# Prompt attention on one core: full-row products with the low parts of the keys, P and its values one point later, sinks copied by ScalarE

## The chip, the cores and the metric

The kernel runs on one core of a Trainium2 chip. The metric is the device time of one execution in microseconds. The core has TensorE (matrix products; PE for the products, PEld for the loads of their stationary operand), VectorE (DVE), ScalarE (ACT), GpSimd (POOL) and SyncE (SP, which issues most of the transfers). They run side by side, each through its own instructions in program order, and wait for each other by semaphores.

## The reference

One layer of a decoder: a prompt of 2048 tokens with 1024 features, and 32 sample rows (8 sequences of 4 tokens) that look at caches. One input projection gives queries, keys and values of two attention branches, and two gates:

```python
qa, ka, va, qb, kb, vb, ga, gb = split(x @ w_in)      # rotary positions on q and k
# A: window 128, 8 query heads, 2 key heads of 64, one learned sink per head
s = where(mask, qa @ ka.T * 64 ** -0.5, -1e30)
m = maximum(max(s), sink)
oa = exp(s - m) / (sum(exp(s - m)) + exp(sink - m)) @ va
# B: three groups of 4 heads, (window, dilation) = (128, 1), (512, 4), (2048, 16)
ob = sum over groups of weight * softmax(qb @ kb.T * 64 ** -0.5) @ vb
x = LN(a * x + (sig(ga) * (oa @ w_a) + sig(gb) * (ob @ w_b)) @ w_o)
x = LN(a * x + (gelu(conv3(x @ w_u)) * (x @ w_v)) @ w_down)
```

In blocks of 128 tokens each query block looks at its own key block and the one before it. In the dilated groups a block consists of tokens 4 or 16 apart; the blocks of the third group, and each fourth of the second, have no block before them.

## The kernel before

All of it is float32. A product of two float32 operands is made as three products of split operands: hi · hi, lo · hi and hi · lo, where hi is ScalarE's rounded copy and lo the difference, made by VectorE (in branch A's splits of x by POOL).

**Phases.** Phase 1 projects and runs the prompt attention (to about 1158 us of the profile), then the gates and the attention of the sample rows (to about 1392 us); phases 2 and 3 are the output projection and the feed-forward.

**Slots.** Phase 1 is a row of slots, one for each tile of 128 tokens and each kind: B0, B1, B2 (the three groups of branch B), A, and G (gates). Each kind has 16 prompt slots (i = 0 to 15) and one of the sample rows (i = 16), which comes last except in G. A slot (`slot`, L352) makes 4 units of 256 columns, 8 steps of 128 rows and 3 products each: 96 products on L379. After every 12 of them there is a *point*, so that a slot has eight. At a point the slot calls `adv` (L381), which runs the next step of every attention job in flight, the newest first; the half projections that are done are taken out of PSUM (`late`, with the rotary arithmetic of `rope`, L427 to L435) at point 6 (point 5 in A) and after the last point:

```python
371                for kh in range(2):
...
381                    self.adv()
382                    if late is not None and (u, kh) == evac_at:
383                        late()
384                        late = None
...
406        if kind[0] == "B":
407            self.drain()
408        late()
```

At points 3 and 7 of B slots (`adv_bg`) one step of the cached-key products of the sample rows also runs on VectorE (L796, L799): 16 steps for each group, in slots 2 to 9 of the next kind (for the third group in A). At point 2 the next tile of x is split (`make_xs`: hi on ScalarE, L41, lo on VectorE, in A on POOL, L42). In B0 the tile of x is transposed there too.

**A job of branch B** (`attn_b`, L622) belongs to tile i and runs in slot i + 1. Its steps, one a point:

1. transposes of q (L630) and of k (L634, into the one bank of `psO`); `split_q` makes the stationary tiles qT[x] (L591, L593): hi in the 64 partitions a head comes in, lo in the other 64; `split_k` makes kH[x], hi twice above each other (L604, L606), and kL, the low parts (L608);
2. split of the values (`split_v`, L442, L445);
3. scores (`qk`, L617 and L619) for two heads of each pair, and the softmax of both pairs (`softmax_pair`: masked maximum L548, its scaled negative nm L552, exponentials L554);
4. nothing;
5. and 6. transposes of the exponentials P (L564), and their split PT (L41 on ScalarE, L42 on VectorE);
7. and 8. products with the values (L658), the first into the bank of `psO`, the second into one of three `psT` banks; `both` adds the two halves of the partitions into O (copy on ScalarE L572, sum on VectorE L573), POOL adds hi and lo (L661), and POOL's queue stores O to d_ob (L662).

With eight steps and eight points a job of branch B ends in its slot, and `drain` finds nothing to run in a plain slot.

The scores:

```python
617                nc.tensor.matmul(dst[x], lhsT=qT[x][:, qi], rhs=self.kH[x][:, ki, sl, :], start=True, stop=False)
618            for x, here, there in self.HALF:
619                nc.tensor.matmul(dst[x], lhsT=qT[x][here, qi], rhs=self.kL[here, ki, sl, :], start=False, stop=True)
```

L617 contracts over 128 rows, (hi + lo of q) · hi of k. L619 contracts over the 64 rows of one half, hi of q · lo of k; its two products lie in different halves of the array. A call makes two of each for each of two rounds r: eight products.

**A job of branch A** (`attn_a`, L665) has twelve steps and lasts one and a half slots, so two jobs are in flight. It calls `qk` twice, at points 3 and 5, and has four softmaxes: two at point 3, one at point 5, one at point 8. Each takes the sink as one more key: L692 copies two sink values (`sk8`) behind the scores in P on VectorE, then come the masked maxima (L694), nm (L697) and the exponentials (L699). P's transposes come at points 5 and 7, and at points 1 and 2 of the next slot; O (tile OA) is collected over points 1 to 4 of the next slot.

**Buffers.** P, PT: two each. O and OA: one tile in a pool of its own. `buf` (L306) is a shared ring of ten tiles of 128 × 512: raw weights and x, rotary temporaries, gates on their way out, cached keys.

Of the kernel before, what the change touches and what calls it, by code (L numbers as in the profile page):

```python
# [7 lines left out]
F32 = mybir.dt.float32  # L8
# [26 lines left out]
class Net:  # L35
# [19 lines left out]
    def unit_list(self):  # L55
        a = self.a
        w_in = a["w_in"][0].rearrange("(k p) n -> p k n", p=128)

        def win(c0):
            return unit(w_in[:, :, c0:c0 + 256])  # L60

        def unit(src):
            """pieces of 512 columns: (place in the unit, source)"""
            kk, n = src.shape[1:]
            if n > 512:
                ps = [((slice(k, k + 1), slice(c, c + 512)), src[:, k:k + 1, c:c + 512]) for k in range(kk) for c in range(0, n, 512)]
            else:
                d = 512 // n
                ps = [((slice(k, min(k + d, kk)), slice(0, n)), src[:, k:min(k + d, kk)]) for k in range(0, kk, d)]
            return kk, n, ps  # L70

        def pair(u, v):
            return 8, 256, [((slice(k, k + 4), slice(c, c + 128)), x[:, k:k + 4]) for c, x in ((0, u), (128, v)) for k in (0, 4)]

        gate = iter(range(8))
        us = []
        for g in range(3):
            us += [win(768 + g * 256), win(1536 + g * 256), win(2304 + g * 256)]
            us.append(win(GATE0 + 256 * next(gate)))
        us += [win(0), win(256), win(512), win(GATE0 + 256 * next(gate))]  # L80
        us += [win(GATE0 + 256 * next(gate)) for _ in range(4)]
        bra = a["w_br_a"][0].rearrange("(k p) n -> p k n", p=128)
        brb = a["w_br_b"][0].rearrange("(k p) n -> p k n", p=128)
        wo = a["w_o"][0].rearrange("(k p) n -> p k n", p=128)
        wo = [unit(wo[:, :, c * 256:(c + 1) * 256]) for c in range(4)]
        us += wo + [unit(bra[:, :, 0:512]), unit(brb), unit(bra[:, :, 512:1024])]
        wup = a["w_up"][0].rearrange("(k p) n -> p k n", p=128)
        wdn = a["w_down"][0].rearrange("(k p) n -> p k n", p=128)
        for _ in GROUPS:
            for ti, (j0, nj) in enumerate(THIRDS):  # L90
                for j in range(j0 + (ti > 0), j0 + nj + (ti < 2)):
                    us.append(pair(wup[:, :, j * 128:(j + 1) * 128], wup[:, :, DFF + j * 128:DFF + (j + 1) * 128]))
                us += [unit(wdn[:, j0:j0 + nj, c * 256:(c + 1) * 256]) for c in range(4)]
        return us

    def prefetch(self, limit=None):
        """raw loads of the next pieces, as many as may wait"""
        if limit is not None:
            self.rawlim = limit
        while len(self.raws) < self.rawlim and self.loaded < self.loadcap and (self.units or self.pieces):  # L100
            self.load_piece()
            self.loaded += 1
# [18 lines left out]
    def unit_steps(self, dst=None, pool=False):  # L121
        """a unit's tile and the steps that fill it"""
        kk, n, np_ = self.shapes.pop(0)
        if dst is None:
            w = self.wp.tile([128, 2, 2048], F32R, tag="w", name="w")
            hi3, lo3 = [w[:, x, :kk * n].rearrange("p (k n) -> p k n", k=kk) for x in range(2)]
        else:
            hi3, lo3 = dst

        def step(q):  # L130
            e = self.nc.gpsimd if pool and q == 1 else None
            r3, _, _, _, (ks, cs) = self.raws.pop(0)
            self.split(hi3[:, ks, cs], lo3[:, ks, cs], r3, e)
            self.prefetch()

        return (hi3, lo3), [lambda q=q: step(q) for q in range(np_)]

# [39 lines left out]
    # ==== phase 1: projections and prompt attention =======================  # L177
# [174 lines left out]
    def slot(self, kind, i, t, xs, units, prep, after_unit, rp):  # L352
# [53 lines left out]
        if kind[0] == "B":  # L406
            self.drain()
# [29 lines left out]
    def split_v(self, src):  # L437
        """hi and lo of the values beside each other for each head, two heads to a tile"""
        vs = []
        for c in range(src.shape[1] // 128):  # L440
            v = self.at.tile([128, 2, 2, 64], F32R, tag="vr", name="vr", bufs=4)
            self.nc.scalar.activation(v[:, :, 0], src[:, c * 128:(c + 1) * 128].rearrange("p (v d) -> p v d", v=2), AF.Copy)  # L442
            vs.append(v)
        for c, v in enumerate(vs):
            self.nc.vector.tensor_tensor(v[:, :, 1], src[:, c * 128:(c + 1) * 128].rearrange("p (v d) -> p v d", v=2),  # L445
                                         v[:, :, 0].bitcast(F32), ALU.subtract)
        return vs
# [95 lines left out]
    def softmax_pair(self, sps, nk, mask, m, nm, den, cols, accum=True, init=None):  # L543
        """exp of two heads' scores; m, nm, den: [128, n] tiles, cols: their two columns"""
# [13 lines left out]
    def transpose_p(self, P, order):  # L558
        """hi and lo of the transposed exponentials"""
# [9 lines left out]
    def both(self, O, ops, x):  # L569
        """the sum of the products with hi and lo values, which come in the two halves of the partitions"""  # L570
# [5 lines left out]
    def keys(self, n, has_prev):  # L576
        """slots of the ring, mask, number of key blocks and whether this tile's come first"""
# [7 lines left out]
    def split_q(self, q3):  # L585
        """hi and lo of a head's queries above each other; the hi half is the half that the head comes in"""
# [9 lines left out]
    def split_k(self, k3, cur):  # L596
        """hi of a head's keys twice above each other, and lo in the half that the head comes in"""
        nc = self.nc
        n = k3.shape[1]
        if not hasattr(self, "kH"):  # L600
            self.kH = [self.at1.tile([128, 2, 2, 128], F32R, name="kH%d" % x) for x in range(2)]
            self.kL = self.at1.tile([128, 2, 2, 128], F32R, name="kL")
# [4 lines left out]
        for x, here, there in self.HALF:  # L607
            nc.vector.tensor_tensor(self.kL[here, :n, cur], k3[here], self.kH[x][here, :n, cur].bitcast(F32), ALU.subtract)  # L608

    def qk(self, qT, sl, nk, pairs):  # L610
        """scores of two head pairs: one bank for each half of the partitions"""
        nc = self.nc
        tiles = [self.psS.tile([128, 512], F32, tag="s", name="pss") for _ in range(2)]
        for r, (qi, ki) in enumerate(pairs):
# [3 lines left out]
            for x, here, there in self.HALF:  # L618
                nc.tensor.matmul(dst[x], lhsT=qT[x][here, qi], rhs=self.kL[here, ki, sl, :], start=False, stop=True)  # L619
        return tiles  # L620

    def attn_b(self, kind, i, t):  # L622
# [24 lines left out]
        PTs = []  # L647
        for x in range(2):
            yield
            PTs.append(self.transpose_p(Ps[x], [(c, b) for c in range(2) for b in range(nb)]))  # L650
        O = self.at1.tile([128, 512], F32, tag="O", name="O")
# [13 lines left out]
    def attn_a(self, t):  # L665
# [22 lines left out]
        def softmax(r, x, sps):  # L688
            """exponentials of heads 4x + 2r and the next, the sink as one more key"""
            c = 4 * x + 2 * r  # L690
            P = self.at.tile([128, 2, 257], F32, tag="P", name="P")
            nc.vector.tensor_copy(P[:, :, nk], self.sk8[:, c:c + 2])  # L692
# [43 lines left out]
        O = self.at1.tile([128, 512], F32, tag="O", name="OA")  # L736
# [11 lines left out]
    def store_rec(self):  # L748
        """1 / denominator of branch A, one row for each tile and head"""
# [15 lines left out]
    def sample_scores(self, g):  # L765
        """products of the sample queries of one group with its cached keys: [slot, (h, b, t)]"""
# [35 lines left out]
    def sample_attn(self):  # L802
# [20 lines left out]
        # branch A: queries of one cache row at a time, the others' columns zero  # L823
# [26 lines left out]
        # rows (h, b, t): keys of all groups side by side  # L850
# [60 lines left out]
        # values of branch B: rows (hi/lo, 16 tokens, h) of two halves of the tokens side by side;  # L911
        # the columns of other tokens in the stationary operand are zero
# [72 lines left out]
        # feature-major: the sum of both parts, one head in each half of the partitions  # L985
# [55 lines left out]
    # ==== phase 2: branches, gates, output projection, first norm ==============  # L1041
    def lnorm_a(self, z, np_):
        """mean and 1 / standard deviation over the 1024 columns, given in two halves"""
# [21 lines left out]
    def split_mm(self, ps, M, h, l, wh, wl, first, last):  # L1065
        """three products of split operands; of the M sample rows hi and lo are columns of h, and so rows of ps"""
# [4 lines left out]
    def lower(self, ps, M):  # L1071
        """the rows of the lo parts, moved beside those of the hi parts"""
# [14 lines left out]
    def phase2_weights(self):  # L1087
        """w_o over the place of x^T"""
# [12 lines left out]
    def load(self, i):  # L1101
# [3 lines left out]
        if M == 128:  # L1105
# [13 lines left out]
            # the dilated groups are stored one residue after the other  # L1119
# [13 lines left out]
    def conv_consts(self):  # L1133
        """taps and offset of the convolution, one column for each feature block"""
# [168 lines left out]
    # ==== phase 3: gated convolutional feed-forward, second norm ================  # L1303
# [25 lines left out]
    def phase3(self):  # L1329
# [3 lines left out]
        with ExitStack() as st:  # L1333
# [125 lines left out]
            def ln_last(y, bs, x):  # L1459
                """second norm of a tile of the last group, from the statistics of four chunks"""  # L1460
# [131 lines left out]
def consts():  # L1592
    """Tables that depend on shapes alone: rotary cos and sin by row, masks of the key blocks."""
# [38 lines left out]
```

## Time and profile before

| | us |
|---|---|
| median of 3 runs (lowest, highest) | 3319.46 (3315.23, 3322.72) |
| span of the profiled execution | 3319.4 |
| B0 slots, 8.70 to 282.29 us | 273.59 |
| B1 slots, 282.29 to 561.16 us | 278.87 |
| B2 slots, 561.16 to 822.15 us | 260.99 |
| A slots, 822.15 to 1158.30 us | 336.15 |
| G slots, 1158.30 to 1392.00 us | 233.70 |

The profiled execution took as long as the median of the runs. Busy time is the time in which an engine has an instruction in work. In a list of events the columns are start, length (both in us), engine, line, operation, output and inputs, shapes, how many of them in a row, and in brackets the idle time of the engine before it and what ended it. In a line of a stretch the columns are its ends, its length, then for each engine the busy time and the number of instructions (x), the granted TensorE clock, the share of the DMA engines and GB/s. In a list of waits: who waited for whom, total us, how many times, the longest.

### The profile page before, as it was taken

The page shows a single profiled execution, that of the slowest core. Times are in us where ns is not written, and L with a number is a line of the kernel's source. Part 1 is how long each engine was busy: PE and PEld are TensorE (multiplying, and loading weights), DVE is VectorE, ACT ScalarE, POOL GpSimd, SP SyncE. Part 2 cuts the span into 40 slices and gives each one's busy share as a digit, 9 for nine tenths or more (in the row PEclk, how much of TensorE's full clock was granted, in tenths as well). Part 3 has the DMA queues.
Part 4 walks back from the last instruction along what each step waited for, and adds up shares of the span by engine and source line. Part 5 has one row for each costly group of instructions (what it writes and reads, how often), then busy time and mean ns, then how long its engine had stood idle before and what let it go on. Part 6 is the DMA issues. An engine that isn't in the chain of part 4 may idle for free.

```text
span 3319.4 us, 56740 instructions
## 1 busy us (share of the span) xinstructions
PE 3224.0 (97%) x21839; PEld 2918.7 (88%) x21839; DVE 1963.1 (59%) x4094; ACT 1387.6 (42%) x3033; POOL 584.4 (18%) x669
## 2 busy tenths in 40 slices
PE   8999999999999999999999999999999999999999
PEld 8998888988888889878887888889888888999998
DVE  5666776776788733367766444474446544474446
ACT  5555555556555534322224333342333333342332
POOL 1112112222211210245552000030001100030001
PEclk9999999999999999999999999999999999999999
DMA  3112212322221234577755323443234433442231
GB/s 116 53 47 87 72 42 74 101 80 85 69 56 49 61 94 140 163 200 189 182 146 157 119 87 99 121 141 100 83 97 124 141 88 97 122 143 77 80 91 57
DMA packets 480037, 343.03 MB, mean 103 GB/s; under 512 B 113938, under 2 KB 435564, under 8 KB 479766
## 3 DMA queue, kind: packets, MB, share of 16 engines
q1 hardware_dynamic: 462390, 290.78, 31.0%
q0 software_dynamic: 17232, 48.56, 4.6%
q8 instruction: 172, 2.82, 0.4%
q14 instruction: 99, 0.81, 0.1%
q10 hardware_dynamic: 144, 0.07, 0.0%
HBM read 279.71 MB, written 59.59 MB: 102 GB/s over the span
## 4 chain that ended last, share of the span: by engine, by line
PE 59%; DMA 1%; DVE 1%; issue 1%; ACT 0%; POOL 0%; SPq 0%; DVEq 0%; ACTq 0%; POOLq 0%
PE psu L1391 30%; PE psdn L1069 14%; PE psw L1069 5%; PE psb L1069 4%; PE psd L379 4%; PE psdf L1069 1%; DMA oa<-d_oa 1%; PE pso L963 1%; PE pst L1233 0%; PE pst L1268 0%; DMA ob<-d_ob 0%; DMA b<-in_w_o 0%; DVE w L42 0%; DVE y L1442 0%; DMA b<-d_hT 0%
## 5 line engine op out<-in xcount | busy, mean ns | idle before, releaser
L379 PE MATMUL psd<-w,xs 128*128 128x256 f32 x7680 | 1019.2, 286 | 20.5 <-POOL w L42 11.0
L1391 PE MATMUL psu<-h,w 128*128 128x512 f32 (+1 forms) x5280 | 1012.5, 353 | 2.9 <-ACT h L41 2.8
L1391 PEld LDWEIGHTS psu<-h,w 128*128 128x128 f32 x5280 | 860.4, 188 | 149.4 <-ACT h L41 3.8
L379 PEld LDWEIGHTS psd<-w,xs 128*128 128x128 f32 x7680 | 949.3, 190 | 32.9 <-POOL w L42 12.4
L1069 PE MATMUL psdn<-w,gt 128*128 128x256 f32 (+1 forms) x4008 | 476.9, 280 | 1.9 <-DVE y L1442 1.9
L1069 PEld LDWEIGHTS psdn<-w,gt 128*128 128x128 f32 (+1 forms) x4008 | 474.0, 186 | 5.1 <-DVE y L1442 4.3
L42 DVE TENSOR_TENSOR w<-b,w 128x512 fp32r<-128x512 f32 (+1 forms) x613 | 400.8, 712 | 18.1 <-ACT w L41 17.0
L41 ACT ACTIVATE w<-b 128x512 fp32r<-128x512 f32 x636 | 346.5, 607 | 127.5 <-PE psdn L1069 63.9
L1402 ACT ACTIVATE ext<-psu 128x512 f32<-128x512 f32 (+1 forms) x110 | 56.3, 512 | 451.6 <-PE psu L1391 451.5
L1415 DVE SCALAR_TENSOR_TENSOR ac<-ext,cw,ac 128x512 f32<-128x512 f32 (+1 forms) x88 | 71.1, 808 | 286.9 <-ACT ac L1414 286.9
L1442 DVE SCALAR_TENSOR_TENSOR y<-y,psdn 128x256 f32<-128x256 f32 x176 | 73.2, 420 | 275.3 <-PE psdn L1069 271.9
L1069 PE MATMUL psw<-WO,mT 128*128 128x512 f32 (+1 forms) x800 | 189.4, 395 | 0.9 <-DVE mT L42 0.9
L1069 PEld LDWEIGHTS psw<-WO,mT 128*128 128x128 f32 (+1 forms) x800 | 148.5, 186 | 38.9 <-DVE mT L42 1.1
L1411 POOL COPY mix<-ext 128x2 f32<-128x2 f32 x66 | 13.1, 198 | 926.8 <-ACT ext L1402 906.8
L42 DVE TENSOR_TENSOR xs<-R,xs 128x1024 fp32r<-128x1024 f32 x64 | 106.0, 1656 | 115.5 <-ACT xs L41 115.5
L42 DVE TENSOR_TENSOR PT<-pst,PT 128x512 fp32r<-128x512 f32 (+1 forms) x160 | 96.5, 610 | 103.5 <-ACT PT L41 102.0
L1069 PE MATMUL psb<-w,oT 128*128 128x512 f32 (+1 forms) x600 | 149.2, 407 | 6.6 <-ACT b L451 5.1
L41 ACT ACTIVATE gt<-ac 128x512 fp32r<-128x512 f32 x110 | 58.3, 549 | 222.5 <-DVE ac L1422 162.7
L1069 PEld LDWEIGHTS psb<-w,oT 128*128 128x128 f32 (+1 forms) x600 | 113.6, 192 | 35.6 <-ACT b L451 5.8
L554 ACT ACTIVATE P<-P,nm 128x256 f32<-128x256 f32 (+1 forms) x192 | 86.4, 451 | 125.2 <-issue 89.5
L564 PE MATMUL pst<-idn,P 128*128 128x128 f32 x548 | 102.5, 284 | 33.0 <-ACT P L554 23.0
L661 POOL TENSOR_TENSOR O<-O 64x256 f32<-64x256 f32 x96 | 77.5, 807 | 226.5 <-DVE O L573 226.5
(258 smaller groups left out, 3703.4 us busy)
## 6 DMA issues: line engine op xcount, KB each, us to landing
b<-in_w_up SPq DMA_DIRECT2D x352, 256.0 KB, 4.0
b<-in_w_down SPq DMA_DIRECT2D x160, 256.0 KB, 3.5
b<-in_w_in SPq DMA_DIRECT2D x80, 256.0 KB, 4.0
b<-in_x_prompt SPq DMA_DIRECT2D x64, 256.0 KB, 4.3
b<-in_cache_b SPq DMA_DIRECT2D x64, 256.0 KB, 3.1
ga<-d_gate SPq DMA_DIRECT2D x32, 512.0 KB, 5.8
b<-d_q SPq DMA_DIRECT2D x48, 256.0 KB, 4.2
d_gate<-b SPq DMA_DIRECT2D x64, 128.0 KB, 1.9
```

Of the source, the lines that this page charges most:

```text
L41: self.nc.scalar.activation(hi, src, AF.Copy)
L42: (eng or self.nc.vector).tensor_tensor(lo, src, hi.bitcast(F32), ALU.subtract)
L379: nc.tensor.matmul(dst, lhsT=l, rhs=r[:, k, :], start=(k == 0 and q == 0), stop=(k == 7 and q == len(ops) - 1))
L554: nc.scalar.activation(P[:, x, :nk], P[:, x, :nk], AF.Exp, bias=nm[:, c:c + 1], scale=SCALE, accum_out=den[:, c:c + 1])
L564: nc.tensor.transpose(ps[:, n * 128:(n + 1) * 128], P[:, x, b * 128:(b + 1) * 128], self.idn)
L661: nc.gpsimd.tensor_tensor(o[:, :, 0], o[:, :, 0], o[:, :, 1], ALU.add)
L963: nc.tensor.matmul(oB[:, hf * 256:(hf + 1) * 256], lhsT=l, rhs=V[:, q, t * 256:(t + 1) * 256], start=(n == 0 and q == 0), stop=(n == len(p ...
L1069: self.nc.tensor.matmul(ps[:x.shape[1]], lhsT=x, rhs=w, start=(first and q == 0), stop=(last and q == len(ops) - 1))
L1391: nc.tensor.matmul(ps[:, :b1 - b0], lhsT=w[:, k, c0:c0 + 128], rhs=h[:, x, k, b0:b1], start=(k == 0 and q == 0), stop=(k == 7 and q == 2))
L1402: nc.scalar.activation(ext[:, 2 + b0:2 + e1], ps[:, 0:e1 - b0], AF.Copy)
L1415: nc.vector.scalar_tensor_tensor(ac[:, :L], ext[:, 1:1 + L], cw[:, 1, j:j + 1], ac[:, :L], ALU.mult, ALU.add)
L1442: nc.vector.scalar_tensor_tensor(y[x][:M, cs], y[x][:M, cs], ALPHA if first else 1.0, ps[:M], ALU.mult, ALU.add)
```

## The change

- `split_k`, `qk`: kL becomes two tiles of 128 partitions. The low parts stand in the half that the head comes in, the other half is zeroed once by POOL. L619 contracts over all 128 rows.
- `attn_b`: one more empty step ahead of the transposes of P. They come at points 6 and 7, the first values group at point 8, the second at point 1 of the slot after. The drain at the end of B slots goes.
- O and OA come from the shared ring of ten.
- `attn_a`: ScalarE copies the sinks into P.

Comments are taken out as well; the diff without them:

```diff
-        if kind[0] == "B":
-            self.drain()
         late()
...
     def split_k(self, k3, cur):
-            self.kL = self.at1.tile([128, 2, 2, 128], F32R, name="kL")
+            self.kL = [self.at1.tile([128, 2, 2, 128], F32R, name="kL%d" % x) for x in range(2)]
+            for x, here, there in self.HALF:
+                nc.gpsimd.tensor_copy(self.kL[x][there].rearrange("p k s d -> p (k s d)"), self.zero[there].to_broadcast([64, 512]))
...
-            nc.vector.tensor_tensor(self.kL[here, :n, cur], k3[here], self.kH[x][here, :n, cur].bitcast(F32), ALU.subtract)
+            nc.vector.tensor_tensor(self.kL[x][here, :n, cur], k3[here], self.kH[x][here, :n, cur].bitcast(F32), ALU.subtract)
...
     def qk(self, qT, sl, nk, pairs):
-                nc.tensor.matmul(dst[x], lhsT=qT[x][here, qi], rhs=self.kL[here, ki, sl, :], start=False, stop=True)
+                nc.tensor.matmul(dst[x], lhsT=qT[x][:, qi], rhs=self.kL[x][:, ki, sl, :], start=False, stop=True)
...
     def attn_b(self, kind, i, t):
         PTs = []
+        yield
         for x in range(2):
             yield
             PTs.append(self.transpose_p(Ps[x], [(c, b) for c in range(2) for b in range(nb)]))
-        O = self.at1.tile([128, 512], F32, tag="O", name="O")
+        O = self.buf()
...
     def attn_a(self, t):
-            nc.vector.tensor_copy(P[:, :, nk], self.sk8[:, c:c + 2])
+            nc.scalar.activation(P[:, :, nk], self.sk8[:, c:c + 2], AF.Copy)
...
-        O = self.at1.tile([128, 512], F32, tag="O", name="OA")
+        O = self.buf()
```

## The prediction

> **What bounds the kernel now.** I read the page first, then the length of single slots, then the waits of TensorE in the projection phase, and last the order of events in one slot on each engine.
>
> ```profile
> span 3319.4 us, 56740 instructions
> PE 3224.0 (97%) x21839; PEld 2918.7 (88%) x21839; DVE 1963.1 (59%) x4094; ACT 1387.6 (42%) x3033; POOL 584.4 (18%) x669
> ```
> TensorE is busy for 97% of the span, so its time is the kernel's time, unless other engines make it wait. The four lines below are one slot each of kinds B0, B1, B2 and A (start and end, length, busy time by engine).
>
> ```profile
> 171.72:187.70 15.98, 15.98 (x134) 15.43 (x133) 9.80 (x27) 9.49 (x24) 2.74 (x4) 1.00 0.17 55
> 399.12:415.88 16.76, 15.75 (x127) 14.77 (x125) 13.18 (x31) 9.36 (x22) 3.13 (x4) 1.00 0.26 68
> 764.51:779.82 15.31, 14.65 (x119) 13.88 (x118) 9.47 (x27) 8.70 (x23) 3.29 (x5) 1.00 0.12 40
> 957.59:977.59 20.00, 19.52 (x152) 17.55 (x151) 16.38 (x44) 11.38 (x31) 3.67 (x3) 1.00 0.18 52
> ```
> In B0 TensorE never stops. In B1, B2 and A it is idle for 0.5 to 1.0 us of each slot. The waits of TensorE (us in total, times, longest) say for what, first those up to 1330 us, then those of the A slots alone:
>
> ```profile
> PE pst L564 <- ACT P L554: 23.0, 30, 1.0
> ```
> ```profile
> PE pst L564 <- ACT P L699: 8.2, 30, 1.4
> ```
> The transposes of P wait for the exponentials, in branch B and in A. Now TensorE in the B1 slot, and the score products of the B0 slot:
>
> ```profile
> 400.54 0.38 PE L630 MATMUL pst<-idn,q 128*128 128x128 f32 x2
> ...
> 403.82 0.40 PE L617 MATMUL pss<-kH,qT 128*128 128x256 f32 x2
> 404.15 0.58 PE L619 MATMUL pss<-kL,qT 64*128 64x256 f32 x2
> 404.66 0.51 PE L617 MATMUL pss<-kH,qT 128*128 128x256 f32 x2
> 405.09 0.38 PE L619 MATMUL pss<-kL,qT 64*128 64x256 f32 x2
> 405.41 3.10 PE L379 MATMUL psd<-w,xs 128*128 128x256 f32 x24
> 409.46 0.93 PE L564 MATMUL pst<-idn,P 128*128 128x128 f32 x4 [0.95 <-ACT P L554]
> ...
> 413.99 1.59 PE L379 MATMUL psd<-w,xs 128*128 128x256 f32 x12
> 415.40 0.64 PE L658 MATMUL pso<-PT,vr 128*128 128x256 f32 x4
> ```
> ```profile
> 177.28 0.40 PE L617 MATMUL pss<-kH,qT 128*128 128x256 f32 x2
> ...
> 178.67 3.11 PE L379 MATMUL psd<-w,xs 128*128 128x256 f32 x24
> ```
> Twelve projection products take 413.99 to 415.40 = 1.41 us, 0.118 us from start to start. Eight score products would take 0.94 at that pace. They take 403.82 to 405.41 = 1.59 in B1 and 177.28 to 178.67 = 1.39 in B0. So going from 128 rows to 64 and back costs 0.65 and 0.45 us, and about 0.10 more on the first product behind (24 products then show 3.10, where 12 show 1.59 and 12 more should add 1.41).
>
> The other engines of the B1 slot, ScalarE and then VectorE:
>
> ```profile
> 401.82 0.77 ACT L604 ACTIVATE kH<-pst 64x256 fp32r<-64x256 f32 x2
> ...
> 414.24 0.59 ACT L572 ACTIVATE O<-pso 64x512 f32<-64x512 f32 x1 [1.28 <-PE pso L658]
> ```
> ```profile
> 407.75 0.41 DVE L548 CUSTOM_DVE_ANT_0 P<-pss,mk 128x256 f32<-128x256 f32 x1
> ...
> 411.40 0.69 DVE L42 TENSOR_TENSOR PT<-pst,PT 128x512 fp32r<-128x512 f32 x1 [0.47 <-ACT PT L41]
> ...
> 413.60 0.41 DVE L427 TENSOR_TENSOR q<-psd,cs 128x256 f32<-128x256 f32 x1
> ...
> 415.65 0.68 DVE L573 TENSOR_TENSOR O<-pso,O 64x512 f32<-64x512 f32 x1
> 416.25 0.67 DVE L796 TENSOR_TENSOR b<-b 128x512 f32<-128x512 f32 x1
> 416.96 0.69 DVE L799 TENSOR_REDUCE S<-b 128x8 f32<-128x512 f32 x1
> ```
> The softmax starts at 407.75, 2 us after the scores: ScalarE and VectorE first finish the splits of q, k, v and of the next x, in order. So a chain runs from the transposes of q (400.54) over these splits to the first P (409.46), 8.92 us, whatever TensorE does between.
>
> **The change part by part.**
>
> *Full rows.* Score calls fall to eight equal products. TensorE saves 0.45 + 0.10 = 0.55 us a call in B0 and 0.65 + 0.10 = 0.75 in B1. The zero halves are written once on POOL beside the first slots, three points ahead of their first use: nothing. The Trainium skill (TensorEngine Tiling, Key Properties) has a rule against this part: tiles of different rows work in parallel. The trace agrees (two 0.38 us products in 0.38 us at 405.09); by that rule alone, full rows add 160 pairs × 0.118 = 19 us, an estimate. The same section says that a change of tiling mode drains the array, and 1.59 against 0.94 shows the drain to be the larger.
>
> *One point later (B).* The P transposes get 12 more projection products ahead of them; the second values group goes behind the transposes of the next slot's q and k. In program order ScalarE's copy of that group's O (0.59) now stands behind the copies of q and k and in front of the splits of v and x: it was ahead of the chain and is now in it. So the chain becomes 8.92 + 0.59 = 9.51 us. TensorE's own path over the same stretch is 8.92 − 0.95 (wait) − 0.75 + 1.41 + 0.47 (values, 4 × 0.118) = 9.1. So P stays late, by about 0.4 instead of 0.95. From P to the next q there is one point less, 1.41 + 0.47. A B1 slot so changes by 0.59 − 1.88 = −1.29; a B2 slot, with half the values, by 0.59 − 1.41 − 0.24 = −1.06. In B0 there was no wait and the split of x is shorter (P was just on time): TensorE stays the bound, −0.55.
>
> With that group move its sum and its store on POOL's queue, behind the store of k and v in B2. POOL is busy for about 3 us of such a slot, and nobody but a later reuse of the buffer waits for the store: nothing. The drain that goes had nothing left to run in a plain slot, where eight points finish a job; behind a sample slot its three steps fit in the eight points too: nothing.
>
> *A new wait.* The transposes of k write the one psO bank, which the first values group now leaves only one point earlier. After P's transposes in B1 VectorE does PT (411.40, that is 1.94 behind 409.46) 0.69, rotary q and k 2.05 (413.60 to 415.65), the second PT 0.69, the O sum 0.69: free at 6.06. TensorE comes there 415.40 − 409.46 = 5.94 behind P plus 0.22 for q, at 6.16: no wait, with 0.1 to spare. But in slots 2 to 9 of B1 and B2 the cached-key products of the sample rows (416.25 and 416.96, 1.43 together) stand between: free at 7.5, TensorE waits 1.3 us. Behind it queue the split of k and the chain; k's copies started 401.82 − 400.54 = 1.28 behind q, at 7.22, and now start at about 7.5 + 0.45 = 7.95. So these slots gain 1.29 − 0.73 = 0.56 in B1, and some 0.75 in B2, whose PTs are half as long (estimate).
>
> *Sinks on ScalarE (A).* VectorE's copy of two elements takes 2.32 us in each A slot; it ends as POOL's split of x ends:
>
> ```profile
> 965.72 2.40 POOL L42 TENSOR_TENSOR xs<-R,xs 128x1024 fp32r<-128x1024 f32 x1
> 965.82 2.32 DVE L692 COPY P<-sk 128x2 f32<-128x2 f32 x1
> ```
> ```profile
> 846.37 2.38 POOL L42 TENSOR_TENSOR xs<-R,xs 128x1024 fp32r<-128x1024 f32 x1 [7.71 <-ACT xs L41]
> ...
> 848.25 0.51 DVE L697 TENSOR_SCALAR nm<-m 128x2 f32<-128x2 f32 x1
> ```
> ```profile
> L697 DVE TENSOR_SCALAR nm<-m x64: 169/169/511, 848.3 to 1163.0; 128x2 f32<-128x2 f32 x64
> ```
> The copy goes, but two steps on in the softmax comes nm, another small VectorE operation, and in the one slot where it met POOL's split it ended with it too (848.76 and 848.75), three times its median of 0.169. So the wait moves to nm. What is gained is the two maxima that now run ahead of the wait instead of behind it, 2 × 0.41 by the B row plus their read-outs, 0.9 us (estimate). The sink copies cost ScalarE between nothing (it is busy for 11.38 of 20.00) and 4 × 0.38 (half a kH row each); with two elements in place of 256 I take nothing. The A slots are one closed chain over ScalarE, POOL and VectorE (exponentials, splits, POOL's x, nm, exponentials), so 20.00 becomes 19.1, although TensorE's path alone would allow 20.00 − 0.48 − 2 × 0.65 = 18.2. TensorE's waits for P in A then grow, to some 0.9 a slot.
>
> The Trainium skill (SBUF — State Buffer, Who interferes with whom) calls this an exclusive lock on a port pair, which both copy and tensor_scalar can take; the 848.25 row agrees. If the copy alone took it, A slots would end near 18.4, the lower end of my own range.
>
> *O in the shared ring of ten.* One buffer of the ring is held over two points. In most slots fewer than ten are in use: nothing. Where weights are loaded (slots 16 and 0) a piece may come later or the slot gain by the shorter scores; bounds −4 to +6 us over the four changes of kind, taken as −1.5.
>
> **Sum.** B0: 14 × 0.55 + 1.3 (slot 15 already splits B1's x) = 9.0. B1: five plain slots × 1.29, six with sample work × 0.56, four of one key block (two × 1.06, two × 0.75) = 13.4. B2: eight × 0.75 + six × 1.06 + 0.7 = 13.1. A: 14 × 0.9 + 0.7 = 13.3. Changes of kind 1.5. Together 50.3; 3319.4 − 50 = 3269. The profiled span is the median of the runs (3319.46), so nothing is to be added. Phases behind A do not change.
>
> **Rivals.**
> *All of TensorE's time comes through:* the O copy and the lock hide, no wait at psO. Each slot then loses its idle time and its score excess: B0 9 in all, B1 (1.01 + 0.75) × 11 + (0.66 + 0.65) × 4 = 25, B2 1.31 × 15 = 20, A (0.48 + 1.3) × 14 = 25, kinds 1.5: 3319 − 80 = 3239. For it: 97% busy. Against it: the softmax starts 2 us after the scores.
> *Half the gain:* the chains of B1 and B2 are longer by another 0.6 us (VectorE at 13.18 of 16.76 has little room), and A gains 0.4: 9 + 6 + 6 + 6 = 27, so 3292.
> *Slower:* psO is late in every B slot, not only those with sample work. The spare 0.1 us is small; if VectorE reached the O sum 2.1 us later, TensorE would wait 2 us in 30 more slots, −50 + 60 + 8 (the 16 others by 0.5 more): 3337. It decides from about 1.6 us in each of the 30; against it, nothing of that length stands on VectorE's queue there outside the sample work.
> *It does not do what it says:* the row change costs nothing and P's waits only move: 3319 within 6.
>
> **How the numbers follow.** My forecast 0.60, with a range of its own of 3253 to 3284 (A by nm's lock or without it −10, changes of kind, the ±0.3 us a slot of psO). All through 0.14, half 0.17, no effect 0.04, slower 0.05. What a measurement can tell here is about 0.2%, 6.6 us: faster 0.91, same 0.04, slower 0.05. For 8 in 10 the range reaches into both neighbours, to 3238 and 3296.
>
> **What would show it.** L619 with 128 rows and 0.118 us apart, score calls of about 0.95 us. B0 slots 15.4. L630's follower L634 waiting for DVE O at 1.3 us in about 16 slots. P waits in B about halved, in A doubled. L692 on ACT, and L697 with a median far above 0.17 in a quarter of its uses. It is wrong if L634 waits in plain slots too, if the A slots fall below 18.6 or stay at 20, or if the span of a part behind A moves.

## The result, and the profile after

The changed kernel takes 3259.19 us (median; 3257.96 to 3261.32), the kernel before 3320.49 us beside it on the same chip. The ratio is 0.9817, 95% interval 0.9803 to 0.9831: 61 us less, where 50 were forecast. The page of the changed kernel begins:

```profile
span 3258.2 us, 56718 instructions
...
PE 3175.0 (97%) x21839; PEld 2907.4 (89%) x21839; DVE 1947.6 (60%) x4030; ACT 1397.0 (43%) x3097; POOL 565.5 (17%) x671
```
TensorE's share is as high as before. One slot each, in the columns used before: a slot of B0, a plain one of B1, one of B1 with sample work, one of B2 with sample work, a plain one of B2, and one of A.

```profile
165.70:181.13 15.43, 15.43 (x134) 15.38 (x133) 9.67 (x26) 9.61 (x24) 2.75 (x4) 1.00 0.18 57
461.15:476.68 15.53, 15.03 (x127) 14.58 (x125) 10.55 (x27) 9.67 (x23) 3.26 (x5) 1.00 0.12 40
336.41:352.44 16.03, 15.05 (x126) 14.54 (x125) 13.04 (x31) 9.68 (x23) 3.26 (x5) 1.00 0.29 88
639.46:653.91 14.45, 13.92 (x119) 13.57 (x117) 11.95 (x32) 8.77 (x23) 3.26 (x5) 1.00 0.38 115
725.94:740.27 14.33, 14.11 (x119) 13.71 (x117) 9.39 (x28) 8.75 (x23) 3.26 (x5) 1.00 0.13 43
947.30:966.33 19.03, 18.68 (x152) 17.59 (x150) 15.19 (x40) 11.76 (x35) 3.66 (x3) 1.00 0.21 53
```
Before, they were 15.98, 16.76 (both sorts of B1), 15.34 and 15.31 (B2 with sample work and plain) and 20.00. What is left of TensorE's waits up to 1280 us (lines have moved by two or one: P's transposes are L562, the exponentials L552 in B and L700 in A, the sum of O L571, the products with values in A L713):

```profile
PE pst L634 <- DVE b L571: 11.7, 19, 0.9
PE pso L659 <- DVE PT L42: 7.0, 6, 1.9
PE pso L713 <- DVE PT L42: 6.1, 17, 2.0
...
PE pst L562 <- ACT P L552: 4.0, 12, 0.7
...
PE pst L562 <- ACT P L700: 1.5, 6, 0.4
...
PE psd L379 <- POOL w L42: 0.7, 1, 0.7
```
The waits for P fell from 23.0 to 4.0 us in B, and from 8.2 to 1.5 in A. The new wait is at the top: k's transposes (L634) wait for the sum of O. The second line lies at the changes of kind alone, two waits at the end of each group of B, where the products with values wait for PT (2.1 us in five waits before). In the B1 slot at 336.41, TensorE, VectorE and ScalarE around it:

```profile
337.09 0.68 DVE L797 TENSOR_TENSOR b<-b 128x512 f32<-128x512 f32 x1
...
337.81 0.69 DVE L800 TENSOR_REDUCE S<-b 128x8 f32<-128x512 f32 x1
337.83 0.38 PE L630 MATMUL pst<-idn,q 128*128 128x128 f32 x2
...
338.41 0.67 DVE L571 TENSOR_TENSOR b<-pso,b 64x512 f32<-64x512 f32 x1
...
339.14 0.44 PE L634 MATMUL pst<-idn,kv 128*128 128x128 f32 x2 [0.93 <-DVE b L571]
...
342.73 0.40 PE L617 MATMUL pss<-kH,qT 128*128 128x256 f32 x2
...
343.68 4.42 PE L379 MATMUL psd<-w,xs 128*128 128x256 f32 x36
```
The sample rows' products (337.09 and 337.81) stand ahead of the sum of O, as the prediction had it. Of the 19 waits, 16 are in slots 2 to 9 of B1 and B2 and three, of 0.25 to 0.31 us, around the last slot of a kind; plain slots have none. The score call takes 342.73 to 343.68, 0.95 us (1.59 before).

In the A slot at 947.30, POOL's split of x, VectorE's nm and the exponentials behind it:

```profile
955.37 2.39 POOL L42 TENSOR_TENSOR xs<-R,xs 128x1024 fp32r<-128x1024 f32 x1
...
956.38 1.40 DVE L698 TENSOR_SCALAR nm<-m 128x2 f32<-128x2 f32 x1
957.88 0.52 ACT L700 ACTIVATE P<-P,nm 128x257 f32<-128x257 f32 x1 [2.50 <-DVE nm L698]
```
Three of the slot's four nm take 0.17; this one ends at 957.78, as POOL's split ends at 957.76. Of the 64 nm, 15 are long, one for each of 15 splits of POOL (1.40 to 1.42 us in thirteen), and each ends within 0.04 us of its split. The sink copy (L693, at 955.18) costs ScalarE 0.20.

The changes of kind gained most over their forecast. Three slots each (the last and two first of a kind; at the end of A two), before and after, us:

| | before | after | one point later alone |
|---|---|---|---|
| B0 to B1 | 48.27 | 45.40 | 45.99 |
| B1 to B2 | 48.66 | 45.21 | 45.94 |
| B2 to A | 47.29 | 44.17 | 44.86 |
| A to G | 41.63 | 38.74 | 41.63 |

Before, POOL's queue in the first B1 slot:

```profile
286.58 1.18 POOL L661 TENSOR_TENSOR O<-O 64x256 f32<-64x256 f32 x1
289.17 0.72 POOL L661 TENSOR_TENSOR O<-O 64x256 f32<-64x256 f32 x1 [1.42 <-DVE O L573]
290.19 0.74 POOL L662 DMA_DIRECT2D d_ob<-O  x1 [0.29 <-POOL O L661]
291.00 6.69 POOL L42 TENSOR_TENSOR w<-b,w 128x512 fp32r<-128x512 f32 x2
```
And what the projection waited for those splits in phase 1, before:

```profile
PE psd L379 <- POOL w L42: 11.0, 7, 3.2
```
POOL in the same slot after:

```profile
279.37 0.73 POOL L662 TENSOR_TENSOR b<-b 64x256 f32<-64x256 f32 x1 [1.83 <-DVE b L571]
280.07 1.28 POOL L42 TENSOR_TENSOR w<-b,w 128x512 fp32r<-128x512 f32 x1
282.96 1.17 POOL L662 TENSOR_TENSOR b<-b 64x256 f32<-64x256 f32 x1 [1.62 <-DVE b L571]
...
285.24 1.80 POOL L42 TENSOR_TENSOR w<-b,w 128x512 fp32r<-128x512 f32 x1
```
Before, two splits of weights stood behind both sums of O and the store, and took 6.69 us together, while VectorE split weights and x; the projection waited 3.2 us for them at each change inside B and into A. After, the first of them comes between the sums (1.28 us), the second behind the store (1.80): 0.7 us of waiting is left in all.

### The profile page after: what moved, and what is told of

It reads as the page before. It is cut to its first block, busy times and chain, and to the rows that moved or that the text cites. A ratio compares the mean times of both kernels' runs of the same rounds, so it can differ in the third digit from the quotient of the medians.

```text
span 3258.2 us, 56718 instructions
## 1 busy us (share of the span) xinstructions
PE 3175.0 (97%) x21839; PEld 2907.4 (89%) x21839; DVE 1947.6 (60%) x4030; ACT 1397.0 (43%) x3097; POOL 565.5 (17%) x671
## 4 chain that ended last, share of the span: by engine, by line
PE 58%; issue 2%; DMA 2%; DVE 1%; SPq 0%; ACT 0%; POOL 0%; DVEq 0%; POOLq 0%; ACTq 0%
PE psu L1392 31%; PE psdn L1070 14%; PE psw L1070 5%; PE psb L1070 4%; PE psd L379 2%; PE psdf L1070 1%; DMA oa<-d_oa 1%; PE pst L1234 0%; PE pso L964 0%; PE pst L1269 0%; DMA ob<-d_ob 0%; DMA ga<-d_gate 0%; DMA b<-in_w_o 0%; SPq L1126 0%; DMA b<-in_w_br_b 0%
## 5 line engine op out<-in xcount | busy, mean ns | idle before, releaser
L379 PE MATMUL psd<-w,xs 128*128 128x256 f32 x7680 | 1001.1, 285 | 8.7 <-ACT w L41 4.0
L552 ACT ACTIVATE P<-P,nm 128x256 f32<-128x256 f32 (+1 forms) x192 | 86.4, 451 | 123.1 <-issue 87.4
L662 POOL TENSOR_TENSOR b<-b 64x256 f32<-64x256 f32 x96 | 71.3, 742 | 337.4 <-DVE b L571 337.4
L41 ACT ACTIVATE xs<-R 128x1024 fp32r<-128x1024 f32 x80 | 116.2, 1452 | 0.9 <-ACT b L756 0.4
```

Source lines behind the costliest of these rows:

```text
L41: self.nc.scalar.activation(hi, src, AF.Copy)
L379: nc.tensor.matmul(dst, lhsT=l, rhs=r[:, k, :], start=(k == 0 and q == 0), stop=(k == 7 and q == len(ops) - 1))
L552: nc.scalar.activation(P[:, x, :nk], P[:, x, :nk], AF.Exp, bias=nm[:, c:c + 1], scale=SCALE, accum_out=den[:, c:c + 1])
L662: nc.gpsimd.tensor_tensor(o[:, :, 0], o[:, :, 0], o[:, :, 1], ALU.add)
```

## The experiments

**The four parts, each alone on the kernel before** (which took 3319.05 us beside them).

*Full rows.* The edits of `split_k` and `qk`, and O in the ring:

```diff
-                nc.tensor.matmul(dst[x], lhsT=qT[x][here, qi], rhs=self.kL[here, ki, sl, :], start=False, stop=True)
+                nc.tensor.matmul(dst[x], lhsT=qT[x][:, qi], rhs=self.kL[x][:, ki, sl, :], start=False, stop=True)
```


> The kernel before with full-row low parts alone (O from the shared ring, for which SBUF has no other room). My theory: TensorE saves 0.55 to 0.75 us in each of 80 score calls, but in B1, B2 and A a chain over ScalarE and VectorE sets the slot, so there the saving turns into longer waits for P. B0 slots 15.98 to 15.45; B1 plain slots stay at 16.7 with the wait for P growing from 0.95 to about 1.6; B2 stays at 15.3; A stays within 0.3 of 20.0. In all -9 to -14 us. Rival (each TensorE microsecond counts): all 80 calls come through, -45 to -55 us, waits for P as before.

Measured: 3318.32 us, ratio 0.9998 (0.9989 to 1.0008): nothing. My expectation of 9 to 14 us fell, and so did the rival's 45 to 55. One slot of B0 and one of B1, and the waits up to 1330 us:

```profile
171.36:187.35 15.99, 15.90 (x134) 15.46 (x133) 9.79 (x27) 9.48 (x24) 2.74 (x4) 1.00 0.18 55
350.42:367.19 16.77, 15.23 (x126) 14.59 (x125) 13.17 (x31) 9.67 (x23) 3.67 (x5) 1.00 0.26 84
```
```profile
PE pst L564 <- ACT P L554: 35.1, 30, 1.5
```
The slots are as long as before. In B1 the longest wait for P grew from 1.0 to 1.5, by what the scores had saved. In B0 no wait is shown, but the transposes of P take longer, first before, then with full rows:

```profile
181.62 0.60 PE L564 MATMUL pst<-idn,P 128*128 128x128 f32 x4
```
```profile
180.94 0.93 PE L564 MATMUL pst<-idn,P 128*128 128x128 f32 x4
181.62 1.08 PE L379 MATMUL psd<-w,xs 128*128 128x256 f32 x7
```
From their start to that of the next product it is 0.36 us before (181.62 to 181.98) and 0.68 now. The 24 products ahead of them took 178.67 to 181.62 = 2.95 before and 177.91 to 180.94 = 3.03 now, although the 0.10 behind the scores is gone. Together that is about the 0.55 that was saved. P had been just on time: the slot was bound by the chain too.

*One point later.* O stays in its own tile.

```diff
-        if kind[0] == "B":
-            self.drain()
...
         PTs = []
+        yield
```


> The kernel before with the extra point and without the drain alone (O in its own tile). My theory: the waits for P go, since 12 products and a values group now cover a chain that is 0.59 longer: B1 plain 16.75 to 15.7, B1 with sample work about 16.1 with a wait at the transposes of k, B2 15.3 to 14.6, B0 and A as before: -20 to -26 us without the changes of kind. If POOL's weight splits at the changes of kind gain by the later store (the 3.2 us waits of the projection for POOL's w go), some 8 us more. Rival (the waits only move to psO or to the values): within 8 us of before.

Measured: 3289.14 us, 0.9908 (0.9893 to 0.9923), 30 us less. B1 plain slots 15.52, B2 plain 14.31, B0 16.03, A 19.99, and the three changes of kind in the table above. Half of the whole gain is this one edit, and that without the shorter scores.

*Sinks on ScalarE.*

```diff
-            nc.vector.tensor_copy(P[:, :, nk], self.sk8[:, c:c + 2])
+            nc.scalar.activation(P[:, :, nk], self.sk8[:, c:c + 2], AF.Copy)
```


> The kernel before with the sinks on ScalarE alone. My theory: the wait for POOL's split of x moves from the copy to nm (nm about 1.4 us once a slot), P comes 0.9 us earlier, and the A slots fall from 20.0 until TensorE binds, at about 19.4 to 19.5: -6 to -9 us. Rival (the copy alone was held): nm stays at 0.17, A slots also end at TensorE's 19.4, so it is told apart by nm's length and by the exponentials' start (2.3 instead of 0.9 earlier).

Measured: 3304.87 us, 0.9957 (0.9942 to 0.9971), 14 us less. The A slot is 19.01, not 19.4 to 19.5, although the kernel before showed only 0.48 us of idle time there. The rows say why. TensorE ahead of P's transposes, in the kernel before:

```profile
967.94 1.58 PE L379 MATMUL psd<-w,xs 128*128 128x256 f32 x12
969.83 0.33 PE L564 MATMUL pst<-idn,P 128*128 128x128 f32 x1 [0.31 <-ACT P L699]
970.32 0.55 PE L564 MATMUL pst<-idn,P 128*128 128x128 f32 x3 [0.16 <-ACT P L699]
970.63 0.36 PE L617 MATMUL pss<-kH,qT 128*128 128x256 f32 x1
```
With the sinks on ScalarE:

```profile
999.96 1.58 PE L379 MATMUL psd<-w,xs 128*128 128x256 f32 x12
1001.38 0.60 PE L564 MATMUL pst<-idn,P 128*128 128x128 f32 x4
1001.74 0.48 PE L617 MATMUL pss<-kH,qT 128*128 128x256 f32 x2
```
From start to start the stretch took 970.63 − 967.94 = 2.69 before and 1.78 now: 0.91 us lost, of which the brackets show 0.47. The ends of products are shown past the start of the next one (1.58 for what takes 1.42), so part of a wait is hidden in the group ahead of it.

*O in the ring of ten.*

```diff
-        O = self.at1.tile([128, 512], F32, tag="O", name="O")
+        O = self.buf()
...
-        O = self.at1.tile([128, 512], F32, tag="O", name="OA")
+        O = self.buf()
```


> The kernel before with O from the shared ring alone. My theory: nothing in plain slots, within 3 us in all. Rival: the ring is what takes away the waits for POOL's weight splits in the first slots of B1, B2 and A, 3.2 us each: -8 to -12 us, or it delays loads by as much.

Measured: 3317.96 us, 0.9998 (0.9988 to 1.0007). Nothing, as costed.

The parts add up to 30 + 14 + 1 + 1 = 46 us, the whole gives 61. So the full rows had to be worth something beside the other parts.

**The changed kernel without the full rows** (kernel before: 3319.23 us, for this and the next three).

```diff
-                nc.tensor.matmul(dst[x], lhsT=qT[x][:, qi], rhs=self.kL[x][:, ki, sl, :], start=False, stop=True)
+                nc.tensor.matmul(dst[x], lhsT=qT[x][here, qi], rhs=self.kL[here, ki, sl, :], start=False, stop=True)
```


> The changed kernel with the 64-row products back, the rest of the change kept. After the run of the rows alone (nothing gained) my theory is: rows pay only where TensorE sets the slot, and with the extra point that is B0. B0 plain slots go back from 15.46 to 16.0, B1 and B2 plain slots stay within 0.05 of 15.51 and 14.33, A within 0.1 of 19.02: 8 to 12 us longer than the changed kernel, near 3269. Rival: rows are worth nothing here either (within 3 us); or all 80 calls count (45 us).

Measured: 3269.19 us, 0.9854 (0.9838 to 0.9871): 10 us slower than the changed kernel. The B0 slot:

```profile
169.97:185.99 16.02, 16.02 (x134) 15.44 (x133) 9.69 (x27) 9.62 (x24) 2.74 (x4) 1.00 0.18 55
```
B0 is 16.02 instead of 15.43; plain slots of B1 (15.52), of B2 (14.31) and of A (19.03) are as with full rows. So the full rows pay in B0 (the B0 slots together take 271.0 us without them and 263.4 with them), and only once P comes a point later there. With 10 us for them instead of 1 the parts add up to some 55; the other 6 us of the whole belong to no part that was tried alone, and where they lie stays open.

**k's transposes in a bank of the scores.** It takes away what L634 waits for.

```diff
-        ps = self.psO.tile([128, 512], F32, tag="o", name="pst")
+        ps = self.psS.tile([128, 512], F32, tag="s", name="pst")
```


> The changed kernel with branch B's transposes of k in one of the two score banks instead of the one bank that the first values group uses. My theory: the waits at L634 for O (11.7 us in 19) are this bank's; they go, and the slots with sample work become like the plain ones: B1 16.03 to 15.5, B2 14.45 to 14.33, sample slots -0.3: 5 to 7 us less. Rival: VectorE's own queue sets those slots, the wait turns up one step later (at P or at the values) and the slots stay as they are.

Measured: 3253.77 us, 0.9803 (0.9788 to 0.9817), 5.4 us less than the changed kernel. The B1 and the B2 slot with sample work:

```profile
334.74:350.28 15.54, 15.10 (x127) 14.62 (x125) 13.04 (x31) 9.69 (x23) 3.28 (x5) 1.00 0.31 90
620.93:635.26 14.33, 14.12 (x118) 13.71 (x117) 11.94 (x32) 8.77 (x23) 3.28 (x5) 1.00 0.36 117
```
They are now as long as the plain ones (15.5 and 14.33). Not all of the 5.4 us is the wait's, though: from the changed kernel's profile to this one's, B1 falls by 2.7 and B2 by 0.2, the start by 1.3 and the part behind the gates by 2.2, which this edit doesn't touch. That last part takes from 1921.8 to 1931.1 us in the profiles of the versions here, so a few us of a whole time can't be laid to an edit; slots and phases tell more. The wait of 11.7 us was worth about 3: where it goes, P is late again by 0.4, and at the changes of kind the scores wait for kL (up to 1.1 us).

**nm on ScalarE too**, so that nothing of VectorE's softmax meets POOL's split.

```diff
-            nc.vector.tensor_scalar(nm[:, c:c + 2], m[:, c:c + 2], -SCALE, None, ALU.mult)
+            nc.scalar.activation(nm[:, c:c + 2], m[:, c:c + 2], AF.Copy, scale=-SCALE)
```


> The changed kernel with branch A's nm computed by ScalarE (copy with a scale) instead of VectorE. My theory: nm is held by POOL's split of x for 1.2 us in each A slot, and that delay goes straight through the chain to the slot: exponentials 1.2 us earlier, A slots from 19.02 to TensorE's own 18.2 to 18.4, 9 to 11 us less in all. Rival: the hold only covers something else that ends at the same time (the A slot was the same 19.02 with TensorE idle 0.35 us or not at all), so A slots stay within 0.1 of 19.02.

Measured: 3243.48 us, 0.9772 (0.9758 to 0.9787), 15.7 us less than the changed kernel. A slot of A, and nm:

```profile
938.33:956.32 17.99, 17.95 (x151) 17.57 (x150) 13.87 (x36) 12.48 (x39) 3.68 (x3) 1.00 0.21 56
```
```profile
L698 ACT ACTIVATE nm<-m x64: 186/203/206, 804.6 to 1088.4; 128x2 f32<-128x2 f32 x64
```
No nm is longer than 0.21 us, and TensorE sets the slot. The held nm is thus shown to be what kept A at 19.0. The gain is larger than the 9 to 11 us that I expected: the 18.2 to 18.4 went by the prediction's path of TensorE, which took off only the 0.48 us of idle time that are shown.

**The second copy of O two points later**, to take its 0.59 us out of the chain up to P.

```diff
+            if x:
+                yield
+                yield
             o = self.both(O, ops, x).rearrange("p (c s t) -> p c s t", c=2, s=2)
```


> The changed kernel with the O copy and sum of branch B's second values group two points later, behind the split of x on ScalarE. My theory: this copy (0.59) stands in the chain from q to P; with it gone B1 plain slots go from 15.51 to 15.05 and B2 plain from 14.33 to 14.0, where TensorE binds; slots with sample work stay within 0.15; 3 to 6 us less. Rival: the chain is not through ScalarE there, plain slots stay within 0.05.

Measured: 3295.39 us, 0.9927 (0.9912 to 0.9941): 36 us slower than the changed kernel. ScalarE and VectorE in a B1 slot:

```profile
337.61 0.59 ACT L570 ACTIVATE b<-pso 64x512 f32<-64x512 f32 x1
...
338.24 0.69 DVE L571 TENSOR_TENSOR b<-pso,b 64x512 f32<-64x512 f32 x1 [1.93 <-ACT b L570]
...
342.50 1.66 PE L379 MATMUL psd<-w,xs 128*128 128x256 f32 x12 [0.61 <-DVE b L426]
```
The copy now stands behind the exponentials, and VectorE, with its sum next in order, stood idle for 1.93 us. The rotary arithmetic and PT behind it came late, and TensorE waited for them: 17.74 in slots with sample work in B1. Plain slots did shorten (15.37, 14.23), so the chain was rightly named and the copy wrongly placed.

**Two versions put together** (kernel before: 3320.84 us). The bank and nm:

> The changed kernel with the two edits together that each gained alone: k's transposes of groups of B in the scores' bank, and the negated maxima of A by ScalarE. They act in different phases (samples' slots of B1 and B2; slots of A), so the gains should add: 3243.5 less the 5.4 us that the bank gave = about 3238, ratio 0.9755. Rival: they share a bound (the start of A or the part behind it gives back what comes early); then it stays at 3243.

Measured: 3241.8 us, 0.9763 (0.9749 to 0.9778). Slots of B1 15.54, of B2 14.35, of A 18.0: both edits act where they did alone. The time lies between the two theories (3238 and 3243), nearer to the rival's; a difference of 4 us is within the intervals. The phases settle more: B1 takes 259.8 us (259.9 with the bank alone) and A 301.5 (301.4 with nm alone), so the two gains add there. What is missing in this profile lies in the gates (234.4 against 232.0 and 232.9) and behind them, and why is open.

The same, with ScalarE's copy issued directly behind the split of x and ahead of the exponentials, VectorE's sum behind the softmax:

```diff
+            if x:
+                self.ocopy = lambda here=here, there=there, ops=ops: nc.scalar.activation(O[here], ops[there], AF.Copy)
+                yield
+                yield
+                self.run_ocopy()
...
+            nc.vector.tensor_tensor(O[here], ops[here], O[here], ALU.add)
```
`slot` also calls `run_ocopy` at point 2, behind the split of x; it is empty if the copy has been issued.

> As best_two, and the second values group's copy of O by ScalarE issued directly behind its half of the split of x, ahead of the next exponentials, with VectorE's sum two points later, behind the softmax of the next job. If the chain q, splits, P with the 0.59 us copy in it is what still sets the plain slots of B1 and B2, that chain loses 0.59 us: B1 15.5 to about 15.1 (TensorE's own work), B2 14.3 to about 14.0, some 10 us, 3228. Rival: the later sum of O stands ahead of the rotary embedding and the copies of PT in VectorE's queue, as in the run in which the copy too was later (slots with samples 16.35 us there); then no gain, or slower than best_two by 5 to 30 us.

Measured: 3229.34 us, 0.9725 (0.9708 to 0.9741), 12 us less than without. Slots of B1 with sample work and plain (those of B2 are 13.97 and 13.96):

```profile
333.24:348.17 14.93, 14.89 (x127) 14.62 (x126) 13.18 (x31) 9.69 (x23) 3.24 (x5) 1.00 0.30 94
450.92:465.82 14.90, 14.89 (x126) 14.62 (x125) 10.61 (x27) 9.68 (x23) 3.24 (x5) 1.00 0.13 42
```
0.6 us a slot in B1, the copy's length, and 0.4 in B2. TensorE is busy throughout in B1. This is the fastest version: 91 us below the kernel before, 30 below the changed one.

**One change of rows in a score call instead of two**, on the kernel before: the four 128-row products first, then the four of 64 rows.

```diff
-                nc.tensor.matmul(dst[x], lhsT=qT[x][:, qi], rhs=self.kH[x][:, ki, sl, :], start=True, stop=False)
+                nc.tensor.matmul(dst[x], lhsT=qT[x][:, qi], rhs=self.kH[x][:, ki, sl, :], start=(r == 0), stop=False)
+        for r, (qi, ki) in enumerate(pairs):
+            dst = [tiles[x][:, r * 256:r * 256 + nk] for x in range(2)]
...
-                nc.tensor.matmul(dst[x], lhsT=qT[x][here, qi], rhs=self.kL[here, ki, sl, :], start=False, stop=True)
+                nc.tensor.matmul(dst[x], lhsT=qT[x][here, qi], rhs=self.kL[here, ki, sl, :], start=False, stop=(r == 1))
```


> The kernel before, with each score call's four 128-row products first and its four 64-row products behind them: one change of rows in a call instead of two (which products open the accumulation is changed with it, so the values in the second half tiles need not be the reference's). If a call's excess over 8 x 118 ns is paid at each change of rows, a call of B1 (1.48 us) falls to about 1.2 or less, and the time stays within 3 us of the kernel before, since the slots there are set by the chain up to P. If 64-row products are themselves slow, the call stays at 1.4 to 1.5 us.

Measured: 3318.42 us in one run: no change in time, as for the full rows alone. A call of B1:

```profile
402.93 0.64 PE L617 MATMUL pss<-kH,qT 128*128 128x256 f32 x4
403.50 0.51 PE L621 MATMUL pss<-kL,qT 64*128 64x256 f32 x4
403.93 1.33 PE L379 MATMUL psd<-w,xs 128*128 128x256 f32 x9
```
The call takes 1.00 us instead of 1.59, with the same products; in B0 it takes 0.99 (176.07 to 177.06) instead of 1.39. So the order costs, not the 64 rows. In B0 one round trip between 128 and 64 rows leaves 0.05 of the 0.45 over eight full products, so the second had cost nearly all of it. In B1 the order does something else too. VectorE makes kL there shortly before the call, in the kernel before:

```profile
403.42 0.88 DVE L608 TENSOR_TENSOR kL<-pst,kH 64x256 fp32r<-64x256 f32 x2 [0.71 <-ACT kH L606]
```
The second half of kL is ready at 404.30, and the second product on L619 starts at 404.35, 0.20 after the first; in a plain call of B0, where kL is ready before the call, the two start together. The second product starts 0.055 us behind kL in every call of B1 and B2. No bracket shows this wait. With full rows alone, where no product changes rows, it is still there: in the call at 321.59 the second product on kL starts 0.30 behind the first, at 322.12, and kL is ready at 322.07. In the call above, with the four products on kH first, it is gone. So of the 0.65 in B1 about 0.45 goes with the changes of rows, as in B0, and 0.20 is a wait for VectorE.

## Why the prediction was right, and where it was not

**Full rows.** The size was right (calls of 0.95; B0 15.43), the ground for it only in part. The prediction took B0 for bound by TensorE because its slots showed no idle time. Alone, the full rows gave nothing there: P was just on time, as the prediction notes, and the chain held the slot. They gave their 0.55 only beside the second part, which the sum added as if each stood by itself. And the 0.65 of a call in B1 is not all a price of going from 128 rows to 64: 0.20 of it was the wait for kL. In the changed kernel that wait is gone from the plain calls too, as TensorE comes to the scores later than kL (342.09 against 342.73 in the slot shown). The Trainium skill (TensorEngine Tiling (Array Packing), Key Properties) says that tiles of different rows work in parallel and that a change of mode drains the array. The trace bears out the second, 1.39 against 0.99 us in B0 by the order alone. Of the first it shows no gain here: four 64-row products take 403.93 − 403.50 = 0.43 us, four full ones at 0.118 take 0.47.

**One point later.** Right. B1 plain slots fell by 1.24 (forecast 1.29), B2 by 0.98 (1.06); P stays late by 0.35 to 0.66 in B1 (0.4). That the O copy in the chain is what remains is shown by the last version: 0.6 us a slot when it leaves.

**The new wait at L634.** Right in place, mechanism and number of slots, smaller in size: 0.93 in six B1 slots, about 0.53 in the other ten, where 1.3 was worked out. The B1 slot shown gained 0.73 instead of 0.56, the B2 slot 0.89 instead of 0.75; over the sixteen it is 2.4 us more than forecast.

**Sinks.** Right in the slot (19.02, forecast 19.1) and in the held nm: 1.40 us, ended with POOL's split. The Trainium skill's exclusive lock (SBUF — State Buffer, Who interferes with whom) agrees, and moving nm off VectorE freed the slot to 17.99. Wrong was where TensorE's lost time would show: not as doubled waits for P (they fell to 1.5 us) but as 0.25 us at L713, waiting for PT, and in stretched groups ahead of it.

**The ring.** Nothing, as costed. Behind the gates nothing moved: from the last projection of phase 1 to the end it is 1926.7 us before and 1927.2 after. The slots of the gates, though, which stand behind A too, took 231.9 instead of 234.4, and the prediction had put nothing there. TensorE waited there 1.4 us for a transfer of cached keys (L844) before and doesn't after; in the run with nm on ScalarE it waits 1.3 for it again, so this is no gain to count on.

**Changes of kind: the term that was mis-sized.** Of the 12.3 us gained in the table, the sum held 1.5 and, in the first full slots of B1, B2 and A, 1.06 + 1.06 + 0.9: 4.5 together. Beside those full slots the changes of kind gained 9.3 us, outside the bounds that the prediction gave (4 less to 6 more). The step "its sum and its store on POOL's queue: nothing" looked at plain slots alone. In the slots with weights the sum and store of O stood ahead of POOL's splits of weights, for which the projection waited 11.0 us in seven waits. That the extra point did most of it is shown by that part alone (7.4 us of the 12.3, a first B1 slot of 17.80 against 17.81 in the changed kernel and 18.91 before). At A to G it gave nothing; there 2.1 of the 2.9 us lie in the last slot of A, 20.7 before and 18.6 after, and 18.6 with the sinks on ScalarE alone. That the splits were longer because VectorE's ran beside them (6.69 us for two against 1.28 and 1.80) is read from the rows, and wasn't tried by itself.

Together, by phases: B0 fell by 10.2 us (forecast 9.0), B1 by 16.2 (13.4), B2 by 15.8 (13.1), A by 18.1 (13.3) and the gates by 2.5 (nothing), with 1.5 forecast for the changes of kind, which lie in all of them. The start is 1.1 later and the part behind the gates 0.5 longer: 61.2 between the spans. By causes: 50.3 + 7.8 (changes of kind) + 2.4 (L634) + 1.1 (A, 14 × 0.08) + 1.7 (gates, beside the first slot, which is in the table) − 1.6 = 61.7, half a us over.

## What to carry to other kernels

A full engine is not proof that it is the bound: where a chain ends just as the engine arrives, shortening the engine's work buys nothing until the chain is shortened, so try the parts alone and together. Moving a producer's tail past a point is worth checking on every queue it passes, in the slots that load weights as well as in the plain ones. And a step moved off the critical chain must not leave another engine waiting in order for it: the same copy of O was worth +36 us behind the exponentials and −12 ahead of them.

## What the runs showed of the hardware that was not expected

- In the A slots TensorE's wait for P was shown at about half its length: 0.47 us in brackets, 0.91 from start to start. Such waits are better measured from the starts around them.
- Two round trips between 128 and 64 rows in a call of B0 cost 0.45 us, one costs 0.05, with the same 0.10 on the product behind (24 products in 3.10 to 3.11 us in the kernel before, 0.22 us between the first two starts behind the call in both).
- A tiny VectorE operation of two elements by 128 partitions, 0.17 us alone, took 1.40 and ended with POOL's split in thirteen slots of A; on ScalarE it took 0.20 and never more than 0.21.
- A wait of TensorE can show no bracket at all: in B1 the second product on kL started 0.20 us behind the first, 0.055 behind the end of VectorE's write, and TensorE was shown busy throughout.
